# Two value chunks of an encoder block's input projection as one seven-product column block, with q, k and v kept in DRAM

## The chip, the core and the metric

The kernel runs on one core of a Trainium2 chip. The metric is the device time of one execution in microseconds. Before the change three runs took 2026.24, 2027.93 and 2028.84; the median is 2027.93.

The core has TensorE (PE in the profile: matmuls and transposes, with PEld its weight load), VectorE (DVE), ScalarE (ACT), GpSimd (POOL) and SyncE (SP, which here only issues transfers). Each engine works through its own instructions in the order in which they are written; engines wait for each other by semaphores. Transfers are issued from the queues of SP, ACT and POOL. Matmuls write to PSUM, which has 8 banks of 128 partitions x 512 floats.

## The reference

One layer of an encoder on x of 512 tokens x 2048, all in float32:

```
h = rmsnorm(x, g_mix)
qa, ka, va, qb, kb, vb = split(h @ w_in)         # 8 + 2 + 2 heads of 128 (A), 8 + 8 + 8 heads (B)
a = rmsnorm(mixer_a(qa, ka, va))                  # per-head rms norm of q and k, 2-D axial rotary, softmax
b = rmsnorm(mixer_b(qb, kb, vb))                  # rotary on 32 of 128 dims, three dilated windows merged
x = x + concat(a, b) @ w_out
x = x + swiglu(rmsnorm(x), w_gate_up, w_down)     # inner width 5632
out = rmsnorm(x, g_final)
```

w_in has 4608 columns: qA at 0 (1024 wide), kA and vA at 1024 (256 each), qB at 1536, kB at 2560 and vB at 3584 (1024 each).

## The kernel before, in words

Precision: every float32 factor of a matmul is split into a high part (ScalarE copies it to a rounded type, `split_hi`, line 235) and a low part (VectorE subtracts, `split_lo`, line 240). `mm3` (lines 197 to 199) then makes three matmuls: high x high, high x low, low x high.

Units: the whole program is a list `units`. A plain unit is one 128-row slice of 512 weight columns for all four token tiles: 4 x 3 = 12 matmuls of 512 columns. A plain chunk (`in_chunk`, `add_chunk`) is 16 units with four PSUM banks. The main loop at the end goes through the units; for each it issues loads and weight splits some way ahead (`prepare`: loads up to 24 us of planned time ahead, splits up to 10), then the unit's matmuls, then what hangs on it (`post`, `hooks`), and then takes one task from a list `side`. So the order of every engine's queue is written out by this loop; the durations in it (`UNIT_US`, `COLS_US`) only set how far ahead things are issued.

Stages: (1) in the first chunk (kA and vA) x is loaded in 128-column pieces and transposed on TensorE one step ahead of its use (`x_transposes`); the result is multiplied by g_mix and split to `xT`, and its square is added up on GpSimd, from which eight one-column matmuls (`col_sums`) and a power on GpSimd give the row scale r1. (2) Eight more plain chunks follow: qA (2), vB, two of q and k of B, vB, two more of q and k. Each is evicted from PSUM with the row scale to tiles that stay in SBUF. (3) As soon as q, k, v of a head exist, its attention goes to `side`, one task a unit: transposes of q (`tq`) and k (`tk`), four scores, four transposes of probabilities (`pt`), four products with v (`pv`). For a chunk of qA there are first eight tasks of norm and rotary (`push_norm_rope`, two for each token tile) and two empty tasks. (4) Eight output chunks of 8 units, A then B, with residual and the sums for the next norm. (5) Gate and up projection in 11 column blocks, (6) down projection in 6, and the last norm.

Column block (`ColBlock`): for two weight column groups of 512 and the two halves of the tokens, seven products of a Strassen-Winograd kind (m1 to m7) take the place of eight. A unit (`Cols`) is one product for one pair of 128-row slices: 2 x 3 = 6 matmuls. Before the split VectorE forms sums of weights for four of the seven products (`weights`, line 771); the stationary side, sums of the activations, lies ready in `arena`. Splits of such a unit (lines 734 and 737) go to eight `twins`, so at most eight units ahead. The products accumulate in banks named z, y and x, and are evicted between them. Before the change only stages 5 and 6 use it.

`RAWS` is the number of weight tiles that may be loaded at once for each kind of block.

Of the kernel before, what the change touches and what calls it, by code (L numbers as in the profile page):

```python
# [50 lines left out]
RAWS = {"raw": 6, "craw": 24, "craw40": 23, "draw6": 22, "draw8": 28}  # L51
# [4 lines left out]
EVICT = 6  # L56

# [6 lines left out]
def encoder_block(ctx, tc, x, g_mix, w_in, g_q_a, g_k_a, g_out_a, g_out_b, w_out, g_ffn,  # L64
# [6 lines left out]
    sm = ctx.enter_context(tc.tile_pool(name="small", bufs=1))  # L71
# [14 lines left out]
    def wslot(tag):  # L86
        if tag == "wa":
            ring[0] += 1
            return home(16 + ring[0] % 12)
        return sp.tile([P, 512], F32R, tag=tag, bufs=W_TILES[tag], name=nm("w"))  # L90
# [4 lines left out]
    def small(base, n=4):  # L95
        return sm.tile([P, 16], F32, tag="t", bufs=24, name=nm(base))[:, :n]
# [7 lines left out]
    ident = cp.tile([P, P], F32, name="ident")  # L104
    gm = cp.tile([P, KD], F32, name="gm")
    gf = cp.tile([P, KD], F32, name="gf")
    go = cp.tile([P, KD], F32, name="go")
    mask = cp.tile([P, S + S - P], F32, name="mask")
    ropeb = cp.tile([P, 2, NT, PARTIAL], F32, name="ropeb")
    ones = cp.tile([P, 1], F32, name="ones")  # L110
    mhalf = cp.tile([P, 16], F32, name="mhalf")
    gqk = cp.tile([P, 2, HD], F32, name="gqk")
# [5 lines left out]
    def home(n):  # L118
        return form_tile(n % 7, n // 7).rearrange("p a b -> p (a b)")
# [5 lines left out]
    warm = slot("warm", BF16, (P, 512))  # L125
# [26 lines left out]
    def load_consts():  # L152
        for i, g in enumerate((g_q_a, g_k_a)):
            nc.sync.dma_start(gqk[:, i, :], row_bcast(g, HD))
        yield
# [3 lines left out]
        yield  # L159
        nc.sync.dma_start(ropeb, c_partial)  # L160
        yield
        nc.sync.dma_start(mask, c_mask)
        yield
# [9 lines left out]
    def rsqrt_mean(ss, n, count, name):  # L173
        t = small(name + "m", n)
        nc.vector.tensor_scalar(t, ss, 1.0 / count, EPS, op0=OP.mult, op1=OP.add)
        r = small(name, n)
        nc.gpsimd.tensor_tensor(r, t, mhalf[:, :n], op=OP.pow)
        return r

    def split(src, name, gain=None, between=None, at=None):  # L180
        if at is None:
            hi, lo = slot(name + "h", F32R), slot(name + "l", F32R)
        else:
            hi, lo = home(at), home(at + 1)
# [3 lines left out]
        else:  # L188
            nc.scalar.activation(hi, src, AF.Copy, scale=gain)
            if between is not None:  # L190
                between()
# [62 lines left out]
    xT = [None] * KD  # L254
    ssx = slot("ssx")

    def x_transposes(k):
        ps = bank("xt")
        for t in range(NT):
            nc.tensor.transpose(ps[:, t * P:(t + 1) * P], xs[k][:, t, :], ident)  # L260
        if k == 0:
            xT[k] = split(ps, "xT", gm[:, k:k + 1], at=0)
            nc.scalar.activation(ssx, ps, AF.Square)
        else:
            sq = slot("xsq")
            xT[k] = split(ps, "xT", gm[:, k:k + 1], lambda: nc.scalar.activation(sq, ps, AF.Square), 2 * k)
            nc.gpsimd.tensor_tensor(ssx, ssx, sq, op=OP.add)
# [9 lines left out]
    def make_r1():  # L277
        r1["r"] = rsqrt_mean(col_sums(ssx), NT, D, "r1")
        r1["rs"] = small("r1s")
# [4 lines left out]
    def push_tables():  # L284
        for i, name in enumerate(("k", "q")):
# [15 lines left out]
            side.extend(lambda a=a, f=part: f(a) for a in range(3))  # L301

    def push_norm_rope(q0, dst, t, nh, name):
# [3 lines left out]
        def first():  # L307
            gs = tabs[name][1]
            tmp = st["tmp"] = slot("ra")
            ss = small("ssq")  # L310
# [4 lines left out]
            st["rs"] = rsqrt_mean(ss[:, :nh], nh, HD, "rq")  # L315
# [7 lines left out]
        def second():  # L323
            gc = tabs[name][0]
# [5 lines left out]
        side.extend((first, second))  # L330

    qA, kA, kTA, vA = {}, [], {}, {}
    vB, qkB = {}, {}
    kTA_done = []

    def post_kvA(ps):
        for j in range(2):
            vA[j] = tuple(home(48 + 2 * j + i).rearrange("p (a b) -> p a b", a=2) for i in range(2))
        for t in range(NT):
            r = r1["r"][:, t:t + 1]  # L340
            k0 = slot("kA")
            src = ps[t][:, 256:]
            h, l = vA[t // 2]
            nc.scalar.activation(h[:, t % 2, :], src, AF.Copy, scale=r)
            nc.scalar.activation(k0[:, :256], ps[t][:, :256], AF.Copy, scale=r)
            nc.vector.scalar_tensor_tensor(l[:, t % 2, :], src, r, f32(h[:, t % 2, :]), op0=OP.mult, op1=OP.subtract)
            kA.append(k0)
        for t in range(NT):
            push_norm_rope(kA[t][:, :256], kA[t][:, 256:], t, NKV, "k")
        wait(1)  # L350
        for kv in range(NKV):
            side.append(lambda kv=kv: transpose_k_a(kv))

    def transpose_k_a(kv):
# [3 lines left out]
        kTA[kv] = split(ps, "kT", at=52 + 2 * kv)  # L358

    def post_qA(j, ps):  # L360
        for t in range(NT):
            q0 = slot("qA")
            nc.scalar.activation(q0, ps[t], AF.Copy, scale=r1["r"][:, t:t + 1])
            push_norm_rope(q0, q0, t, 4, "q")
            qA[j, t] = q0
        wait(2)
        for h in range(4):
            push_head(("A", 4 * j + h))

    def post_vB(j, ps):  # L370
        for t in range(NT):
            r = r1["r"][:, t:t + 1]
            h, l = home(32 + 2 * (NT * j + t)), home(33 + 2 * (NT * j + t))
            nc.scalar.activation(h, ps[t], AF.Copy, scale=r)
            nc.vector.scalar_tensor_tensor(l, ps[t], r, f32(h), op0=OP.mult, op1=OP.subtract)
# [753 lines left out]
```

## Time and profile before

| | us |
|---|---|
| median of three runs | 2027.93 |
| the profiled execution | 2026.94 |
| its span, first to last instruction | 2025.2 |
| TensorE busy | 2005.7 |
| VectorE busy | 1474.1 |
| ScalarE busy | 1051.6 |
| GpSimd busy | 134.9 |

The span is that of one profiled execution. A group's row gives line, engine, operation, output and inputs, count, then busy time and the mean in ns of one. A row of the timeline gives start and duration in us, then engine, line, operation, count, and in brackets how long the engine had been idle and who ended it. A row of a window gives the window, its length, then for PE, PEld, DVE, ACT and POOL the busy time with the number of instructions, then TensorE's granted clock, the share of the 16 DMA engines and GB/s. Neighbouring instructions of one engine overlap a little, so starts tell more of the rate than durations. A row of waits gives who waited for whom, us in total, times, and the longest.

### The profile page before, as it was taken

The page shows a single profiled execution, that of the slowest core. Times are in us where ns is not written, and L with a number is a line of the kernel's source. Part 1 is how long each engine was busy: PE and PEld are TensorE (multiplying, and loading weights), DVE is VectorE, ACT ScalarE, POOL GpSimd, SP SyncE. Part 2 cuts the span into 40 slices and gives each one's busy share as a digit, 9 for nine tenths or more (in the row PEclk, how much of TensorE's full clock was granted, in tenths as well). Part 3 has the DMA queues.
Part 4 walks back from the last instruction along what each step waited for, and adds up shares of the span by engine and source line. Part 5 has one row for each costly group of instructions (what it writes and reads, how often), then busy time and mean ns, then how long its engine had stood idle before and what let it go on. Part 6 is the DMA issues. An engine that isn't in the chain of part 4 may idle for free. (4 is left out here: it accounts for less than half of the span.)

```text
span 2025.2 us, 26727 instructions
## 1 busy us (share of the span) xinstructions
PE 2005.7 (99%) x9123; PEld 1652.5 (82%) x9123; DVE 1474.1 (73%) x2596; ACT 1051.6 (52%) x1872; POOL 134.9 (7%) x149
## 2 busy tenths in 40 slices
PE   9999999999999999999999999999999999999997
PEld 7888888888888888888888888888888887788885
DVE  5555755554754688878877878878779987887876
ACT  5324344443543565555555555555556665666655
POOL 3100100000000000000000000000000121111121
PEclk9999999999999999999999999999999999999998
DMA  7322322223433546657558567467477799768754
GB/s 236 106 80 70 98 74 73 79 78 96 147 113 130 205 142 217 206 167 267 193 195 267 166 222 255 152 221 253 153 253 254 207 248 265 205 158 256 212 124 165
DMA packets 210360, 354.90 MB, mean 175 GB/s; under 512 B 19072, under 2 KB 63920, under 8 KB 210224
## 3 DMA queue, kind: packets, MB, share of 16 engines
q1 hardware_dynamic: 189440, 304.10, 45.9%
q0 software_dynamic: 12544, 25.17, 7.0%
q10 hardware_dynamic: 8240, 23.93, 3.5%
q8 instruction: 71, 1.16, 0.2%
q14 instruction: 65, 0.53, 0.1%
HBM read 300.97 MB, written 52.17 MB: 174 GB/s over the span
## 5 line engine op out<-in xcount | busy, mean ns | idle before, releaser
L734 ACT ACTIVATE tw<-raw 128x512 fp32r<-128x512 f32 x924 | 559.3, 628 | 442.5 <-DVE raw L771 280.7
L737 DVE TENSOR_TENSOR tw<-raw,tw 128x512 fp32r<-128x512 f32 x924 | 619.1, 686 | 173.4 <-ACT tw L734 169.5
L197 PE MATMUL zc<-tw,arena 128*128 128x512 f32 x1056 | 416.1, 394 | 2.0 <-ACT ev L907 1.9
L198 PE MATMUL zc<-tw,arena 128*128 128x512 f32 x1056 | 413.6, 392 | 3.5 <-DVE tw L737 3.5
L199 PE MATMUL zc<-tw,arena 128*128 128x512 f32 x1056 | 413.1, 391 | 0.0
L771 DVE TENSOR_TENSOR raw<-raw,raw 128x512 f32<-128x512 f32 x528 | 361.3, 684 | 0.5 <-DMA raw<-in_w_gate_up_dram 0.5
L198 PEld LDWEIGHTS zc<-tw,arena 128*128 128x128 f32 x1056 | 199.3, 189 | 46.7 <-DVE tw L737 6.5
L197 PEld LDWEIGHTS zc<-tw,arena 128*128 128x128 f32 x1056 | 199.1, 189 | 43.9 <-ACT ev L907 3.0
L199 PEld LDWEIGHTS zc<-tw,arena 128*128 128x128 f32 x1056 | 199.1, 189 | 41.5
L197 PE MATMUL pj<-w,arena 128*128 128x512 f32 x576 | 229.0, 398 | 1.2 <-ACT w L235 1.2
L198 PE MATMUL pj<-w,arena 128*128 128x512 f32 x576 | 224.8, 390 | 0.9 <-DVE w L240 0.9
L199 PE MATMUL pj<-w,arena 128*128 128x512 f32 x576 | 225.5, 391 | 0.1
L198 PE MATMUL yc<-tw,arena 128*128 128x512 f32 x528 | 206.0, 390 | 0.8 <-DVE tw L737 0.8
L197 PE MATMUL yc<-tw,arena 128*128 128x512 f32 x528 | 206.8, 392 | 0.0
L199 PE MATMUL yc<-tw,arena 128*128 128x512 f32 x528 | 205.8, 390 | 0.0
L240 DVE TENSOR_TENSOR w<-raw,w 128x512 fp32r<-128x512 f32 x176 | 130.8, 753 | 21.4 <-ACT w L235 13.6
L908 POOL DMA_DIRECT2D x1d<-ev x76 | 67.4, 990 | 1155.3 <-ACT ev L907 1149.4
L235 ACT ACTIVATE w<-raw 128x512 fp32r<-128x512 f32 x176 | 106.5, 627 | 56.1 <-PE pj L199 32.0
L199 PEld LDWEIGHTS pj<-w,arena 128*128 128x128 f32 x576 | 108.2, 188 | 23.9 <-DVE arena L192 0.5
L197 PEld LDWEIGHTS pj<-w,arena 128*128 128x128 f32 x576 | 108.3, 188 | 23.6 <-ACT w L235 1.4
L198 PEld LDWEIGHTS pj<-w,arena 128*128 128x128 f32 x576 | 108.5, 188 | 23.2 <-DVE w L240 1.2
L198 PEld LDWEIGHTS yc<-tw,arena 128*128 128x128 f32 x528 | 99.2, 188 | 21.8 <-DVE tw L737 1.6
(189 smaller groups left out, 2539.0 us busy)
## 6 DMA issues: line engine op xcount, KB each, us to landing
raw<-in_w_gate_up_dram SPq DMA_DIRECT2D x616, 256.0 KB, 4.5
raw<-in_w_down_dram SPq DMA_DIRECT2D x176, 256.0 KB, 6.7
forms<-pair SPq DMA_DIRECT2D x22, 896.0 KB, 5.2
raw<-in_w_in_dram SPq DMA_DIRECT2D x38, 512.0 KB, 3.7
x1d<-ev POOLq DMA_DIRECT2D x76, 256.0 KB, 6.6
fr<-forms ACTq DMA_DIRECT2D x35, 512.0 KB, 4.5
raw<-in_w_in_dram SPq DMA_DIRECT2D x68, 256.0 KB, 3.0
raw<-in_w_out_dram SPq DMA_DIRECT2D x32, 512.0 KB, 4.9
```

Source lines behind the costliest of these rows:

```text
L197: nc.tensor.matmul(dst, ah, bh, start=start, stop=False, skip_group_check=chained)
L198: nc.tensor.matmul(dst, ah, bl, start=False, stop=False, skip_group_check=chained)
L199: nc.tensor.matmul(dst, al, bh, start=False, stop=stop, skip_group_check=chained)
L235: nc.scalar.activation(self.w[0], src, AF.Copy)
L240: nc.vector.tensor_tensor(self.w[1], self.src, f32(self.w[0]), op=OP.subtract)
L734: nc.scalar.activation(self.pair[:, 0], self.src, AF.Copy)
L737: nc.vector.tensor_tensor(self.pair[:, 1], self.src, f32(self.pair[:, 0]), op=OP.subtract)
L771: nc.vector.tensor_tensor(t[dst], t[src[0]], t[src[1]], op=OP.add if form == "m6" else OP.subtract)
L908: nc.gpsimd.dma_start(x1_dram[2 * cb + j, row], e, accum_op=OP.add)
```

## The change

Input projection: after the first plain chunk (kA, vA) the two chunks of vB become one column block (`in_block`), with the order of products m1, m2, m7, m6, m5, m4, m3. Then come six plain chunks: qA (2) and four of q and k of B. For the block the activations' sums are needed, so in the first chunk each transposed x is copied to a tile (`xpair`, three buffers, one for a pair of steps), split into `arena`, and two steps after the second of a pair VectorE makes four sums and, a step later, ScalarE and VectorE split two of them (`x_sums`, `x_split`). One of these overwrites a quarter of x, which is saved to DRAM by POOL's queue before (`ar_dram`) and brought back after m7.

Row scale: the squares are taken on ScalarE from x loaded once more in rows (`load_rows` in steps 8 to 11, two buffers of 1 MB; `row_squares` in steps 11 to 14). The squares on ScalarE and their sum on GpSimd for each step, and the eight column-sum matmuls, go.

q, k, v: every chunk is evicted and stored to DRAM (`spill`) and loaded again by SP's queue when attention needs it (`reload`, `load_vB`); the split of v is made then.

Attention: all heads are one list. Each task is a slot s: transposes of the probabilities of slot s - 6, product with v of slot s - 7, score of slot s, and the q and k transposes of the head of slot s + 3. Each task has a cost; a unit gives 1.13 credit during the remaining plain chunks and 1.6 during A's output chunks, and tasks are taken while the credit lasts. The tables, k and v of A come after the block, the rest after the first chunk of qA.

Small tiles are packed into fewer buffers, and `RAWS` is 21 in place of 23 and 22 for the last gate and up block and the first down blocks.

```diff
-RAWS = {"raw": 6, "craw": 24, "craw40": 23, "draw6": 22, "draw8": 28}
+RAWS = {"raw": 6, "craw": 24, "craw40": 21, "draw6": 21, "draw8": 28}
+HEAD_RATE = (1.13, 1.6)
+TURN_LAG = 6
+COLUMN_BLOCKS = 1
...
-            xT[k] = split(ps, "xT", gm[:, k:k + 1], at=0)
-            nc.scalar.activation(ssx, ps, AF.Square)
+            nc.scalar.activation(hi, ps3, AF.Copy, scale=gain)
+            nc.vector.scalar_tensor_tensor(lo, ps3, gain, f32(hi), op0=OP.mult, op1=OP.subtract)
+            nc.scalar.activation(flat, ps, AF.Copy, scale=gain)
         else:
-            sq = slot("xsq")
-            xT[k] = split(ps, "xT", gm[:, k:k + 1], lambda: nc.scalar.activation(sq, ps, AF.Square), 2 * k)
-            nc.gpsimd.tensor_tensor(ssx, ssx, sq, op=OP.add)
+            nc.scalar.activation(flat, ps, AF.Copy, scale=gain)
+            nc.scalar.activation(hi, view, AF.Copy)
+            nc.vector.tensor_tensor(lo, view, f32(hi), op=OP.subtract)
+        if half == 0:
+            hook(k, lambda: nc.gpsimd.dma_start(ar_dram[:, i], arena[0][:, 1, i]))
+        else:
+            hook(k + 2, lambda: x_sums(i))
+            hook(k + 3, lambda: x_split(i))
+
+    def x_sums(i):
+        a_l, a_r, s3, s2, b_l, b_r, s1, s4 = (xpair[i][:, n * 256:(n + 1) * 256] for n in range(8))
+        form_sums(a_l, a_r, b_l, b_r, s1, s2, s3, s4)
+
+    def x_split(i):
+        parts = xpair[i].rearrange("p (f c) -> p f c", c=256)
+        for src, dst in ((parts[:, 2:4], arena[0][:, 1:3, i]), (parts[:, 6:8], arena[1][:, 2:4, i])):
+            nc.scalar.activation(dst[:, :, 0], src, AF.Copy)
+            nc.vector.tensor_tensor(dst[:, :, 1], src, f32(dst[:, :, 0]), op=OP.subtract)
...
+    def load_rows(t):
+        rows[t] = sp.tile([P, D], F32, tag="rows", bufs=2, name=nm("rows"))
+        nc.sync.dma_start(rows[t], x[0, t * P:(t + 1) * P, :])
+
+    def row_squares(t):
+        nc.scalar.activation(rows[t], rows[t], AF.Square, accum_out=ss1[:, t:t + 1])
...
-        r1["r"] = rsqrt_mean(col_sums(ssx), NT, D, "r1")
+        r1["r"] = rsqrt_mean(ss1, NT, D)
...
+    def post_plain(name, ps):
+        for t in range(NT):
+            e = slot("ev" + name)
...
+                nc.scalar.activation(e, ps[t], AF.Copy, scale=r1["r"][:, t:t + 1])
+            store(name, t, e, nc.scalar)
+
+    def reload(name, dst):
         for t in range(NT):
+            dst[t] = slot(name)
+            nc.sync.dma_start(dst[t], spill[name][t])
...
+        def task(s):
+            head, i = at(s - TURN_LAG)
+            if head:
+                head.pt(i)
+            head, i = at(s - TURN_LAG - 1)
+            if head:
+                head.pv(i)
...
+            head, i = at(s)
+            if head:
+                head.score(i)
+            head, i = at(s + 3)
+            if head and i == 0:
+                head.tq()
+            if head and i == 1:
+                head.tk()
+        cost = 1.5 if spec[0] == "A" else 1.2
...
+        first = light(0.5, table_tasks() + kn)
+        todo = [weighed(0.1, lambda: reload("qA0", qA[0]))] + light(0.8, q_tasks(0))
+        for h in range(8):
+            todo += head_tasks(("A", h))
...
+    def in_block(names, lo):
+        first = not blocks
+        box = ColBlock(w_in, 0, lo, KD // 2, REREAD, "craw",
+                       chain=("m1", "m2", "m7", "m6", "m5", "m4", "m3") if first else CHAIN)
...
+        rows_of("m1", 0, 0, begin)
+        rows_of("m7", 1, 1, begin)
+        rows_of("m6", 1, 0, begin)
+        rows_of("m2", 0, 0, close)
+        rows_of("m5", 1, 1, close)
+        rows_of("m4", 1, 0, close)
+        rows_of("m3", 0, 1, only)
...
+    last.after("m7", 1, lambda: nc.gpsimd.dma_start(arena[0][:, 1], ar_dram))
+    last.after("m5", 0, load_consts)
+    last.after("m5", 3, lambda: reload("kvA", kA))
+    last.after("m3", 0, lambda: side.extend(first_tasks))
...
+            if 8 <= n < 8 + NT:
+                load_rows(n - 8)
+            if 11 <= n < 11 + NT:
+                row_squares(n - 11)
             if n == KD - 1:
                 make_r1()
             if n + 1 < KD:
-                x_transposes(n + 1)
+                x_prep(n + 1)
...
-        if side:
-            side.popleft()()
+        credit = credit + HEAD_RATE[n >= attend[1]] if attend[0] <= n < attend[2] else 1.0
+        while side and credit >= getattr(side[0], "cost", 1.0):
+            f = side.popleft()
+            credit -= getattr(f, "cost", 1.0)
+            f()
+        if not side:
+            credit = 0.0
```

`begin` evicts a bank with the row scale on ScalarE, `close` adds a second bank to it on VectorE and stores it by POOL's queue, `only` evicts and stores by ScalarE's.

More of the change, by code (lines that the diff above doesn't have):

```diff
@@ L252, in wait, with x_of, x_prep @@
         side.extend([lambda: None] * n)
-    xT = [None] * KD
-    ssx = slot("ssx")
-    def x_transposes(k):
+    xpair = [None] * (KD // 2)
+    ar_dram = dp.tile([P, KD // 2, 2, 256], F32R, tag="ar", name="ar")
+    def x_of(k, t):
+        m = (0, 1, 3, 4)[2 * (k % 2) + t // 2]
+        return cols(tuple(form_tile(m, k // 2)[:, j] for j in range(2)), (t % 2) * P)
+    def x_prep(k):
         ps = bank("xt")
@@ L329, in second @@
                                     st["rs"][:, :, None].to_broadcast([P, nh, HD]), op=OP.mult)
-        side.extend((first, second))
-    qA, kA, kTA, vA = {}, [], {}, {}
+        return [first, second]
+    qA, kA, kTA, vA = {}, {}, {}, {}
     vB, qkB = {}, {}
[L334 to L338, printed above, removed]
-        for t in range(NT):
[L340 to L347, printed above, removed]
-        for t in range(NT):
[L349 to L352, printed above, removed]
+    spill = {name: dp.tile([NT, P, 512], F32, tag=name, name=name)
+             for name in ("kvA", "qA0", "qA1", "vB0", "vB1", "qkB0", "qkB1", "qkB2", "qkB3")}
@@ new lines, in reload, with split_vA @@
+    def reload(name, dst):
+        assert stored[name] == NT, name
+        for t in range(NT):
+            dst[t] = slot(name)
+            nc.sync.dma_start(dst[t], spill[name][t])
+    def split_vA(t):
+        if not vA:
+            for j in range(2):
+                vA[j] = tuple(place(2, 2 * j + i).rearrange("p (a b) -> p a b", a=2) for i in range(2))
+        h, l = (v[:, t % 2, :] for v in vA[t // 2])
+        src = kA[t][:, 256:]
+        nc.scalar.activation(h, src, AF.Copy)
+        nc.vector.tensor_tensor(l, src, f32(h), op=OP.subtract)
@@ new lines, in encoder_block @@
+    last.after("m5", 0, load_consts)
+    last.after("m5", 3, lambda: reload("kvA", kA))
+    last.after("m3", 0, lambda: side.extend(first_tasks))
+    last.after("m3", 0, twins.clear)
+    first_tasks, later_tasks = attention_tasks()
+    attend = [len(units)]
+    queue = side.extend
+    for names, lo in groups[COLUMN_BLOCKS:]:
+        for name, c in zip(names, lo):
+            in_plain(name, c)
+            if queue:
+                hook(len(units) if name == "qA0" else attend[0], lambda: side.extend(later_tasks))
+                queue = None
```

484 lines of the change are left out of this document (263 added, 221 removed).

## The prediction

> **What bounds the kernel now.** First I read the page's head and its busy times, then the windows of the half that the change touches.
>
> ```profile
> span 2025.2 us, 26727 instructions
> PE 2005.7 (99%) x9123; PEld 1652.5 (82%) x9123; DVE 1474.1 (73%) x2596; ACT 1051.6 (52%) x1872; POOL 134.9 (7%) x149
> 300.00:325.00 25.00, 25.00 (x122) 20.66 (x121) 13.35 (x24) 9.97 (x21) 1.29 (x1) 1.00 0.25 74
> 625.00:650.00 25.00, 25.00 (x112) 20.73 (x111) 11.45 (x18) 6.79 (x11) 0.00 (x0) 1.00 0.27 85
> ```
>
> TensorE (PE, first pair of numbers) is busy in both stretches, at a granted clock of 1.00, while VectorE (DVE) and ScalarE (ACT) have room. So in this half a matmul taken away is time gained, unless TensorE then waits for someone. Its own spacing comes from the timeline; between the first two rows lie 45 steps. The other rows are the last step of the first chunk and its end.
>
> ```profile
> 639.67 0.39 PE L198 MATMUL pw<-w,arena 128*128 128x512 f32 x1
> ...
> 649.87 0.39 PE L198 MATMUL pw<-w,arena 128*128 128x512 f32 x1
> 51.55 0.60 PE L260 MATMUL xt<-ident,x 128*128 128x128 f32 x4
> 54.75 0.60 PE L260 MATMUL xt<-ident,x 128*128 128x128 f32 x4
> 55.10 0.48 PE L197 MATMUL pj<-w,arena 128*128 128x512 f32 x1
> 55.65 0.40 PE L199 MATMUL pj<-w,arena 128*128 128x512 f32 x1
> 58.05 1.05 PE L272 MATMUL cs<-ones,ssx 128*128 128x1 f32 x8
> 58.96 0.47 PE L197 MATMUL pj<-w,arena 128*128 128x512 f32 x1
> ```
>
> (649.87 - 639.67) / 45 = 0.2267 us for one matmul of 512 columns. A plain unit has 12 (2.72 us), a unit of a column block 6 (1.36 us), a step of the first chunk with its transposes 3.20 us. What TensorE waited for is short, and the head has two rows of it:
>
> ```profile
> PE pj L197 <- ACT w L235: 1.2, 1, 1.2
> PE pj L198 <- DVE w L240: 0.9, 1, 0.9
> ```
>
> **What is taken away.** Two plain chunks are 2 x 16 x 12 = 384 matmuls; the block has 7 products x 8 pairs x 6 = 336. 48 fewer make 48 x 0.2267 = 10.9 us. The eight column-sum matmuls go too, since the squares are now summed along rows: from 58.05 to 58.96, 0.9 us. The 2.1 us of waits above came behind the old square of x on ScalarE, which is gone; the new copy of x takes its place there. Between 0 and 2.1 I take 1.0. Gains: 12.8 us.
>
> **ScalarE in the first chunk.** Per step it now copies the transposed x (a dependent pair with its high part) and splits a weight, and every second step splits two sums. Then come four squares of 128x2048, in steps 11 to 14, each queued ahead of the next x.
>
> ```profile
> 53.25 0.63 ACT L235 ACTIVATE w<-raw 128x512 fp32r<-128x512 f32 x1
> 55.38 0.69 ACT L189 ACTIVATE arena<-xt,gm 128x512 fp32r<-128x512 f32 x1 [1.50 <-PE xt L260]
> 56.45 1.15 ACT L235 ACTIVATE w<-raw 128x512 fp32r<-128x512 f32 x2
> L689 ACT ACTIVATE arena<-pair 128x1024 fp32r<-128x1024 f32 x8 | 8.4, 1045 | 0.0
> L582 ACT ACTIVATION_READ_ACCUMULATOR j<-x 128x1 f32 x16 | 3.0, 186 | 0.0
> ```
>
> Two independent splits take 1.15, so one adds 0.52. A step costs 0.69 + 0.63 + 0.1 between them + 0.52 + (2 x 0.52) / 2 = 2.46 of 3.20. A square, by the slope from 0.63 (512) to 1.05 (1024), is 0.63 + 3 x 0.42 + 0.19 = 2.08. Four steps then need 4 x 4.54 = 18.2 against 12.8: 5.4 late. How much lateness is free? A step's transposes start at 54.75 and ScalarE 0.63 later, at 55.38; its 0.69 and 0.63, VectorE's 0.69 (next rows) and two hand-overs of 0.1 end 2.84 after the transposes' start. The first matmul that reads the low part is the third of its step, one step on (55.65 for the transposes of 51.55, 4.10): 1.25 free. VectorE's rows:
>
> ```profile
> 53.50 1.30 POOL L267 TENSOR_TENSOR ssx<-ssx,xsq 128x512 f32<-128x512 f32 x1 [1.92 <-ACT xsq L266]
> 54.06 1.28 DVE L240 TENSOR_TENSOR w<-raw,w 128x512 fp32r<-128x512 f32 x1
> 60.44 0.17 DVE L280 TENSOR_SCALAR r1s<-r 128x4 f32<-128x4 f32 x1 [1.14 <-POOL r L177]
> 60.51 0.69 DVE L240 TENSOR_TENSOR w<-raw,w 128x512 fp32r<-128x512 f32 x1
> 658.98 1.56 DVE L660 TENSOR_TENSOR pair<-pair 128x256 f32<-128x256 f32 x4 [3.62 <-ACT pair L682]
> ```
>
> Per two steps it has two low parts of x, two of weights and two of sums at about 0.60 to 0.69 each, and 1.56 of sums: 5.3 of 6.4. But only three pair buffers exist, so the copy of x for step 2i+6 waits for the last split of pair i, and VectorE stands still during copy and high part (1.4): a loop of 5.3 + 1.4 = 6.7, 0.3 more than 6.4, five times; the free 1.25 takes the first two or so, 0.6 stays. TensorE waits 5.4 - 1.25 + 0.6 = 4.7. Bounds: 2.5 (squares run in ScalarE's idle time before their step) to 7 (no slack).
>
> Without POOL's add the weight split is 0.69, not 1.28; I used 0.69. The Trainium skill (GPSIMD Engine Reference, 1. Specifications) says that GpSimd shares its SBUF interfaces with VectorE and contends with two-input instructions, which agrees with these rows; if the eight POOL transfers that now save a half of x did the same, 8 x 0.59 = 4.7 us more of VectorE would come into this chunk. The trace has a split in the middle of two such issues, and it is not stretched:
>
> ```profile
> 1641.58 1.77 POOL L908 DMA_DIRECT2D x1d<-ev  x2 [6.14 <-ACT ev L907]
> 1642.41 0.69 DVE L737 TENSOR_TENSOR tw<-raw,tw 128x512 fp32r<-128x512 f32 x1 [3.36 <-ACT tw L734]
> ```
>
> **From the first chunk into the block.** The row scale now comes after the last square, by way of VectorE's queue and POOL's power (the 1.14 above), so the four evictions start some 1.0 after the chunk's end. Each is 0.69 plus a store issued on ScalarE (0.33, below): 4 x 1.05 = 4.2. Behind them stands the split of the block's fifth unit; only four units of 1.36 (5.4) are split ahead, where before three or four of 2.72 were. High part at 5.2 + 0.6, low part at 6.5, wanted at 5.4 + 0.23: 0.9. Then VectorE still owes two pairs' remains (1.56 + 4 x 0.60 = 4.0) among units that leave it 1.36 - 0.60 = 0.76 each: 4.0 less 3 x 0.76 is 1.7. Together 2.6; bounds 0 and 4. In the block m5 follows m6 in the same banks, so its first matmul waits for the eviction: 0.69 + 0.1 + the matmul's end, less the other bank's 0.68, is 0.4; bound 1.7, the longest such wait below.
>
> **From the block into attention.** q of the first chunk is no longer roped from the eviction but stored, loaded, and then roped. Rows for eviction, store, load and the old rope work:
>
> ```profile
> 104.65 2.73 ACT L363 ACTIVATE qA<-pj,r 128x512 f32<-128x512 f32 x4 [8.16 <-PE pj L199]
> 105.37 0.29 DVE L312 CUSTOM_DVE_ANT_0 ra<-qA 128x128 f32<-128x128 f32 x1 [6.32 <-ACT qA L363]
> 110.42 0.28 DVE L312 CUSTOM_DVE_ANT_0 ra<-qA 128x128 f32<-128x128 f32 x1
> 124.95 1.29 DVE L240 TENSOR_TENSOR w<-raw,w 128x512 fp32r<-128x512 f32 x2
> 133.69 0.60 PE L419 MATMUL qt<-ident,qA 128*128 128x128 f32 x4
> L474 ACTq DMA_DIRECT2D oA<-oT x8: 326/326/357, 178.7 to 383.8; - x8
> oA<-oT ACTq DMA_DIRECT2D x8, 256.0 KB, 2.2
> oback<-oA SPq DMA_DIRECT2D x8, 256.0 KB, 3.0
> ```
>
> The eviction can start 1.8 before the chunk's end F (nine matmuls, less the drain). First store issued at F - 1.1, landed F + 1.1, load landed F + 4.2 to 4.4. VectorE's queue stands at the first rope task until then. A row of q, with two weight splits of 0.60 (1.29 for two, less the overlap) among it, took 110.42 - 105.37, so 3.85 alone; four rows with five weight splits between them are 18.4: done at F + 22.8. The tasks go out at 1.13 per unit and cost 0.8, so the first head's transposes come after the seventh unit, F + 19.0 (before, ten units: 104.65 + 1.8 + 27.2 = 133.7, as the row says). TensorE waits 3.8; bounds 0 and 7 (a load that lands 3 later). The weight splits behind the rope arrive within 0.1 of their need, so nothing else.
>
> For the rest of attention matmuls and transposes are the same, and the cycle uses each probability block six slots after its score. A plain unit with 0.75 slot is about 2.72 + 0.75 x 1.9 = 4.1 of TensorE against VectorE's 0.75 x 2 + 0.6: covered. The old order, with a shorter lag, shows no TensorE wait in this stretch, so I take 0 and move neither end. The tasks weigh about 115, the units give 80 x 1.13 + 32 x 1.6 = 142: the queue empties before B's output chunks. The new reloads are at most 256 KB each where the DMA share is 0.25: 0.
>
> **The smaller weight buffers** (23 to 21, 22 to 21) act in the down projection, where loads are already late:
>
> ```profile
> 1697.74 0.63 ACT L734 ACTIVATE tw<-raw 128x512 fp32r<-128x512 f32 x1 [4.96 <-DMA raw<-in_w_down_dram]
> PE zc L197 <- ACT ev L907: 1.9, 2, 1.7
> ```
>
> One buffer fewer issues a load about a unit (1.36) later, and what ScalarE waits there it hands on in part, since splits run up to eight units ahead. I take 0.5; bounds -1 (another order of loads) and +4 (most of a wait like this one again).
>
> **Sum.** -12.8 + 4.7 + 2.6 + 0.4 + 3.8 + 0.5 = -0.8. The profiled execution took 2026.94 (1.7 around its span); so 2026.1, and as the median of the runs before (2027.93) stands 1.0 above it, 2027.1. All low ends give -10.9 - 0.9 - 2.1 + 2.5 - 1 = -12.4, all high ends -10.9 - 0.9 + 7 + 4 + 1.7 + 7 + 4 = +11.9.
>
> **Rivals.**
> Absorbed waits (faster): rope and block start cost nothing because VectorE gets there in time. For it: the old order left TensorE without a wait at 133.69, and VectorE is at 13.35 of 25 in the attention window. Against: the rope can't start before q is back. -0.8 - 3.8 - 2.6 = -7.2: 2020.7.
>
> The row loads come late (slower). They are four of 1 MB on SP's queue in steps 8 to 11; only two buffers exist, so the third waits for the first square, the fourth for the second, and the block's first weights queue behind them.
>
> ```profile
> raw<-in_w_in_dram SPq DMA_DIRECT2D x12, 512.0 KB, 5.3
> 0.00:60.00 60.00, 56.12 (x268) 43.57 (x269) 34.09 (x47) 30.50 (x56) 20.20 (x20) 1.00 0.70 215
> ```
>
> At 215 GB/s a 512 KB load moves in 2.4 of its 5.3, which leaves 2.9 of landing, and 1 MB moves in 4.9: the third lands 7.8 after its issue, where ScalarE wants it after about 7; the fourth, behind it and two weight loads (2.4), at 4.9 + 2.4 + 4.9 + 2.9 = 15.1, where it is wanted at 11.1 and the first lateness moves that to 11.8: 3.3 late, and ScalarE holds the next x behind it. The weights behind them I put another 3 late. It decides once the fourth lands later than its step, and gives -0.8 + 6.3 = +5.5: 2033.4. Against: 215 is a mean over a window in which the DMA engines were 0.70 busy. The Trainium skill (DMA: Bandwidth & Descriptors, Anatomy of one DMA) gives 2.0 us plus bytes at 436 GB/s, an estimate of 4.4 us for 1 MB: by that the fourth would be in time and this rival void. No row shows a 1 MB load.
>
> The smaller buffers cost a whole late load (slower): +5 in place of 0.5, the 4.96 once more and unshared: 2031.6. Against it: one or two buffers of more than twenty go.
>
> That the change doesn't do what it says (products not fewer) is excluded by the count.
>
> **Chances.** About 0.2%, 4 us, is what can be told from no change. Forecast 0.38 (its own range 2023 to 2031; 0.03 of it faster, 0.02 slower by over 4), absorbed 0.32, late rows 0.24, buffers 0.06 (half of it over 4). So faster 0.35, same 0.36, slower 0.29. The 8-in-10 range, pulled in a little from the two sums of ends, is 2016.5 to 2038.
>
> **What would show it.** Right: 48 fewer 512-column matmuls, gaps of ScalarE's making on TensorE in steps 11 to 14, about 3 us of gaps in the first eight units of the block, one gap of 3 to 4 us before the first q transposes, ended by VectorE. Wrong: a first chunk as even as before's 3.20 a step; ScalarE waiting for row loads; gaps inside the head cycle, which I price at nothing; a longer wait for weights around 1700.

## The result, and the profile after

Five runs of the changed kernel took 2035.35 to 2041.53 us, median 2039.54; five of the kernel before 2026.24 to 2029.18, median 2027.93. The ratio is 1.0055, 95% interval 1.0041 to 1.0070: the change makes the kernel slower by about 11.6 us. The median lies above the range of the prediction (2016.5 to 2038). The profiled execution took 2039.54, with a granted TensorE clock of 0.996 (before: 0.997).

The head of the page after the change:

```profile
span 2037.8 us, 27271 instructions
PE 2004.7 (98%) x9067; PEld 1642.6 (81%) x9067; DVE 1522.5 (75%) x2706; ACT 1093.7 (54%) x1928; POOL 123.2 (6%) x149
```

TensorE has 56 instructions fewer (48 matmuls and 8 column sums), as counted beforehand, and its busy time fell by 1.0, not by 11.8. Where the rest went shows in windows over the part that the change touches. They are cut at the first chunk's end, the first q transposes of after and the output chunks. Columns as in the prediction: window, length, then busy time and count for PE, PEld, DVE, ACT, POOL, then clock, DMA share, GB/s. Before:

```profile
5.00:62.00 57.00, 54.69 (x268) 43.59 (x267) 34.96 (x47) 30.39 (x58) 20.39 (x16) 1.00 0.69 211
62.00:120.00 58.00, 58.00 (x260) 48.02 (x261) 35.54 (x109) 19.05 (x35) 6.26 (x7) 1.00 0.35 100
120.00:225.00 105.00, 105.00 (x495) 86.90 (x494) 55.84 (x112) 42.29 (x89) 2.35 (x2) 1.00 0.25 76
225.00:480.00 255.00, 255.00 (x1213) 210.90 (x1213) 142.81 (x335) 105.17 (x221) 14.60 (x12) 1.00 0.26 81
480.00:625.00 145.00, 145.00 (x696) 119.81 (x695) 83.13 (x173) 68.22 (x135) 9.13 (x7) 1.00 0.43 138
```

And after:

```profile
5.00:62.00 57.00, 54.67 (x259) 42.75 (x258) 37.62 (x71) 45.07 (x74) 4.46 (x8) 1.00 0.93 313
62.00:120.00 58.00, 54.54 (x234) 43.19 (x233) 50.12 (x88) 33.19 (x55) 2.76 (x4) 1.00 0.72 250
120.00:225.00 105.00, 101.86 (x450) 83.93 (x449) 60.92 (x165) 30.25 (x57) 9.44 (x12) 0.98 0.46 157
225.00:480.00 255.00, 253.55 (x1217) 208.32 (x1216) 154.86 (x350) 121.41 (x253) 14.93 (x12) 1.00 0.33 107
480.00:625.00 145.00, 138.30 (x648) 109.79 (x647) 90.43 (x203) 70.03 (x140) 10.43 (x8) 0.98 0.49 158
```

Length less TensorE's busy time is its idle time: before 2.3 in the first window and nothing behind it; after 2.3, 3.5, 3.1, 1.5 and 6.7. Two clocks read 0.98: there some matmuls also ran at half rate (below), which a busy column hides. The largest loss stands in the last window. It holds the end of the input projection and A's output chunks, with heads of B's attention between them: matmuls that the change does not touch. The longest of the waits of after's TensorE up to 660 us name who was late; in the whole list no wait behind the first matmul is ended by a transfer:

```profile
PE qt L474 <- DVE qkB L453: 3.4, 5, 1.2
PE qt L474 <- DVE qA L383: 3.1, 1, 3.1
PE zc L203 <- DVE tw L691: 2.5, 3, 1.9
PE pj L202 <- ACT arena L284: 2.2, 2, 1.2
PE kt L484 <- DVE qTl L194: 1.5, 2, 0.7
```

The first row is the rotary step (here called rope) of B's q and k (`qkB`) on VectorE, ahead of the transposes of q (`qt`). The timeline shows the worst instance:

```profile
532.53 0.16 DVE L502 RECIPROCAL smalls<-smalls 128x1 f32<-128x1 f32 x1 [0.88 <-ACT p L501]
...
533.13 0.35 DVE L449 TENSOR_TENSOR turning<-qkB,fixed 128x64 f32<-128x64 f32 x2
...
534.19 0.33 PE L474 MATMUL qt<-fixed,qkB 128*128 128x128 f32 x1 [1.18 <-DVE qkB L453]
535.12 0.33 PE L474 MATMUL qt<-fixed,qkB 128*128 128x128 f32 x1 [0.60 <-DVE qkB L453]
536.03 0.48 PE L474 MATMUL qt<-fixed,qkB 128*128 128x128 f32 x1 [0.59 <-DVE qkB L453]
536.61 0.29 DVE L453 TENSOR_TENSOR qkB<-qkB,turning 128x128 f32<-128x128 f32 x1
536.96 0.47 PE L474 MATMUL qt<-fixed,qkB 128*128 128x128 f32 x1 [0.45 <-DVE qkB L453]
538.09 0.63 PE L204 MATMUL pw<-arena,arena 128*128 128x512 f32 x1
...
541.92 0.63 PE L204 MATMUL pw<-arena,arena 128*128 128x512 f32 x1
```

The four ropes run from 533.13 to 536.90, 3.8 us, and each transpose stands in TensorE's queue until its own is done: 1.18 + 0.60 + 0.59 + 0.45 = 2.8 us in four waits. VectorE itself had stood idle for 0.88 shortly before (first row), so it was the order of its queue that kept the ropes until then. Then comes what no step of the prediction had: between the last two rows lie nine steps, so (541.92 - 538.09) / 9 = 0.426 us a matmul, not 0.227. The windows around it give the clock:

```profile
210.00:216.00 6.00, 5.29 (x17) 4.22 (x18) 3.15 (x5) 1.64 (x3) 0.00 (x0) 0.72 0.27 84
532.00:537.00 5.00, 2.19 (x9) 0.99 (x8) 4.16 (x19) 2.11 (x5) 0.00 (x0) 0.89 0.27 92
537.00:543.00 6.00, 6.00 (x18) 4.73 (x19) 4.22 (x9) 1.81 (x4) 0.00 (x0) 0.52 0.00 0
543.00:548.00 5.00, 5.00 (x29) 4.14 (x27) 3.08 (x7) 3.50 (x7) 1.29 (x1) 1.00 0.31 105
```

From 537 to 543 TensorE counts as busy all the time, and gets half its clock.

The whole stretch from the first matmul of the input projection to the first of gate and up can be added up from TensorE's timeline, row by row: start to start, less 0.2267 for each matmul of 512 columns; what a row puts down to another engine is a wait, and a spacing of 0.40 to 0.45 without one is half rate.

| us | before | after | difference |
|---|---|---|---|
| matmuls: 2880, 2832 | 652.8 | 641.9 | -10.9 |
| transposes and column sums | 44.3 | 46.2 | +1.9 |
| waits | 2.1 | 16.7 | +14.6 |
| the rest of a gap that has a wait | 0.3 | 3.4 | +3.1 |
| half rate | 0.0 | 3.6 | +3.6 |
| small gaps that no wait explains | 16.4 | 19.7 | +3.3 |
| together | 715.9 | 731.6 | +15.7 |
| from there to the span's end | 1302.4 | 1299.3 | -3.1 |

Waits, rest and half rate by place, before and after: first chunk 2.4 and 2.7; block 0 and 4.0; first q of A 0 and 4.5; 225 to 480 us 0 and 1.7; 480 to 625 us 0 and 10.8. (The last line of the table takes the first `zc` matmul behind the output chunks, below, from the spans.)

```profile
722.77 0.39 PE L197 MATMUL zc<-tw,arena 128*128 128x512 f32 x1
```

```profile
738.48 0.39 PE L202 MATMUL zc<-tw,arena 128*128 128x512 f32 x1
```

So the theory to test: the block saves its 10.9, and the new order of the attention tasks loses about 12.5 in stalls of TensorE, about half of it where two tasks (ropes of B, transposes of B's q) stand too near each other at the quick pace of 1.6 credit a unit. Rivals: the block itself is to blame (ScalarE's squares, VectorE's backlog), or the 10.9 never arrives.

### The profile page after: what moved, and what is told of

The parts are those of the page before. It is cut to its first block, busy times and chain, and to the rows that moved or that the text cites. A ratio compares the mean times of both kernels' runs of the same rounds, so it can differ in the third digit from the quotient of the medians.

```text
span 2037.8 us, 27271 instructions
## 1 busy us (share of the span) xinstructions
PE 2004.7 (98%) x9067; PEld 1642.6 (81%) x9067; DVE 1522.5 (75%) x2706; ACT 1093.7 (54%) x1928; POOL 123.2 (6%) x149
## 5 line engine op out<-in xcount | busy, mean ns | idle before, releaser
L688 ACT ACTIVATE tw<-raw 128x512 fp32r<-128x512 f32 x980 | 593.3, 628 | 467.2 <-DVE raw L725 309.5
L691 DVE TENSOR_TENSOR tw<-raw,tw 128x512 fp32r<-128x512 f32 x980 | 656.3, 687 | 173.4 <-ACT tw L688 169.4
L202 PE MATMUL zc<-tw,arena 128*128 128x512 f32 x1120 | 439.9, 393 | 3.0 <-ACT ev L1045 2.2
L203 PE MATMUL zc<-tw,arena 128*128 128x512 f32 x1120 | 437.7, 391 | 5.0 <-DVE tw L691 4.8
L204 PE MATMUL zc<-tw,arena 128*128 128x512 f32 x1120 | 437.1, 390 | 0.0
L725 DVE TENSOR_TENSOR raw<-raw,raw 128x512 f32<-128x512 f32 x560 | 383.3, 685 | 2.9 <-DMA raw<-in_w_gate_up_dram 2.9
L203 PEld LDWEIGHTS zc<-tw,arena 128*128 128x128 f32 x1120 | 210.6, 188 | 51.5 <-DVE tw L691 9.0
L202 PEld LDWEIGHTS zc<-tw,arena 128*128 128x128 f32 x1120 | 210.7, 188 | 47.6 <-ACT ev L1045 2.9
L204 PEld LDWEIGHTS zc<-tw,arena 128*128 128x128 f32 x1120 | 210.6, 188 | 43.9
L203 PE MATMUL yc<-tw,arena 128*128 128x512 f32 x560 | 218.3, 390 | 1.1 <-DVE tw L691 1.1
L202 PE MATMUL yc<-tw,arena 128*128 128x512 f32 x560 | 219.1, 391 | 0.0
L204 PE MATMUL yc<-tw,arena 128*128 128x512 f32 x560 | 218.1, 389 | 0.0
L202 PE MATMUL pj<-w,arena 128*128 128x512 f32 x448 | 179.0, 399 | 2.4 <-ACT arena L284 2.2
L203 PE MATMUL pj<-w,arena 128*128 128x512 f32 x448 | 175.7, 392 | 0.7 <-DVE w L245 0.7
L204 PE MATMUL pj<-w,arena 128*128 128x512 f32 x448 | 176.1, 393 | 0.0
L203 PEld LDWEIGHTS yc<-tw,arena 128*128 128x128 f32 x560 | 105.2, 188 | 23.8 <-DVE tw L691 2.4
L204 PEld LDWEIGHTS yc<-tw,arena 128*128 128x128 f32 x560 | 105.1, 188 | 22.0
L202 PEld LDWEIGHTS yc<-tw,arena 128*128 128x128 f32 x560 | 105.1, 188 | 21.5
L202 PE MATMUL xc<-tw,arena 128*128 128x512 f32 x280 | 109.2, 390 | 0.0
L203 PE MATMUL xc<-tw,arena 128*128 128x512 f32 x280 | 109.1, 389 | 0.1
L204 PE MATMUL xc<-tw,arena 128*128 128x512 f32 x280 | 109.0, 389 | 0.0
```

Of the source, the lines that this page charges most:

```text
L202: nc.tensor.matmul(dst, ah, bh, start=start, stop=False, skip_group_check=chained)
L203: nc.tensor.matmul(dst, ah, bl, start=False, stop=False, skip_group_check=chained)
L204: nc.tensor.matmul(dst, al, bh, start=False, stop=stop, skip_group_check=chained)
L688: nc.scalar.activation(self.pair[:, 0], self.src, AF.Copy)
L691: nc.vector.tensor_tensor(self.pair[:, 1], self.src, f32(self.pair[:, 0]), op=OP.subtract)
L725: nc.vector.tensor_tensor(t[dst], t[src[0]], t[src[1]], op=OP.add if form == "m6" else OP.subtract)
```

## The experiments

SBUF is so full that most edits only fit with fewer weight tiles for the new block (`craw`). So the control has 20 in place of 24, and every kernel below has it too. Each ratio is to runs of the kernel before on the same chip at the same time; kernels of different groups are compared by these ratios. The first four ran together, the next four, and the last four.

**Control.**

```diff
-RAWS = {"raw": 6, "craw": 24, "craw40": 21, "draw6": 21, "draw8": 28}
+RAWS = {"raw": 6, "craw": 20, "craw40": 21, "draw6": 21, "draw8": 28}
```

> The changed kernel with 20 instead of 24 weight tiles for the column blocks; nothing else. It is the control for the next three, which need the memory. Every theory: within 3 us of the changed kernel (2036.5 to 2042.5), the same TensorE gaps at 207 us (q of A) and between 500 and 605 us (B's heads in A's output chunks).

Measured: 2038.46, ratio 1.0054 (1.0039 to 1.0069), the same as with 24. Its last window:

```profile
480.00:625.00 145.00, 137.88 (x651) 109.52 (x650) 91.19 (x204) 69.93 (x141) 10.43 (x8) 0.99 0.48 156
```

**A steady pace.** The tasks behind the input projection go out at 1.13 a unit, not 1.6.

```diff
-HEAD_RATE = (1.13, 1.6)
+HEAD_RATE = (1.13, 1.13)
```

> As the control, but A's output chunks give 1.13 credit a unit like the plain chunks, not 1.6. Theory pace (B's heads are pushed faster than VectorE's chain of maximum, exponential, normalising and split can follow): the TensorE waits between 500 and 605 us, some 9.7 us, and the half-speed stretch behind them, 2.2 us, go; 2027 to 2030. Theory rope order (the rotary of B's q and k stands straight in front of the transposes that need it): the waits on the rotary, 3.9 us, and the half-speed stretch stay, 2.5 to 5 us are won from the other waits.

Measured: 2032.02, ratio 1.0025 (1.0013 to 1.0036), 6.4 under the control. Two views, the window and the waits:

```profile
480.00:625.00 145.00, 142.84 (x688) 115.81 (x688) 95.29 (x211) 74.36 (x149) 10.46 (x8) 1.00 0.48 155
```

```profile
PE qt L474 <- DVE qkB L453: 1.5, 3, 0.6
```

Idle time in that window fell from 7.1 to 2.2, 37 more TensorE instructions fit into it, and the clock is whole. VectorE does more work there than in the control (95.29 against 91.19), so over the window its throughput was not the limit, as the prediction held. What the slower pace widens is the distance in the queues: the worst transposes of q now start 2.2 us behind the first of their ropes, not 1.06, and wait 0.95, not 3.0. Neither theory on record came out whole: the waits for ropes shrank and did not go, most waits for split probabilities and k went too, and the time stayed above 2027 to 2030.

**A gap behind the first q.** A task that does nothing, weighed 3.4, stands between the ropes of A's first q and the first transposes.

```diff
-        todo = [weighed(0.1, lambda: reload("qA0", qA[0]))] + light(0.8, q_tasks(0))
+        todo = [weighed(0.1, lambda: reload("qA0", qA[0]))] + light(0.8, q_tasks(0)) + [weighed(3.4, lambda: None)]
```

> As the control, but three units without an attention task stand between the rotary of A's first q and its first transposes. Theory: the 3.3 us wait at 207 us goes, and with it the slow matmuls behind it (0.43 us spacing for about 4 us, another 1.9): 5 us faster. Rival (the wait's length is all it costs): 3.3 us faster. Rival (the wait only moves to the next consumer of VectorE): no change.

Measured: 2032.00, ratio 1.0028 (1.0019 to 1.0037), 6.5 under the control. The wait of 3.1 for q of A and the half rate behind it are gone; in its place stands one of 1.1 for a weight split of VectorE. Gate and up begins 6.8 earlier than in the control: 2.8 of that is this wait with its half rate, 1.3 other waits, 1.8 small gaps and transposes, and 0.9 lies ahead of the first input matmul, so it has nothing to do with the edit. The waits in A's output chunks stayed (7.8 against 7.1), on another tensor: the probabilities, up to 2.8 at once.

```profile
PE o L203 <- DVE pTl L194: 3.8, 2, 2.8
PE qt L474 <- DVE qkB L453: 2.0, 3, 1.2
```

**Ropes one slot earlier.**

```diff
-                todo += tasks[:1] + light(0.5, b_ropes(j)) + tasks[1:]
+                todo += light(0.5, b_ropes(j)) + tasks
```

> As the control, but the rotary of B's q and k of the next pair is one slot earlier in the list (before slot 0 of an odd head, not between slots 0 and 1). Theory rope order: the four waits of 2.8 us at 532 to 537 us, the half-speed stretch of 2.6 us behind them, and the smaller one at 442 go: 5 to 6 us faster. Theory pace: VectorE is as late as before, the waits turn up at the probability splits instead, under 2 us won.

Measured: 2035.67, ratio 1.0042 (1.0026 to 1.0059), 2.8 under the control, within what the two intervals leave open, so a gain is not shown. The row `qt <- qkB` is gone; in its place stands

```profile
PE o L203 <- DVE pTl L194: 3.3, 5, 2.5
```

The ropes' 3.8 us of VectorE now delay the low part of a transposed probability block. At a pace of 1.6 they are in somebody's way in both places tried, which fits the larger effect of the pace.

**Squares of 64 columns.** One of the rival's suspects, ScalarE's squares of x, cut to a thirtieth. This kernel leaves most of the sum of squares out, so its row scale is not that of the layer.

```diff
-        nc.scalar.activation(rows[t], rows[t], AF.Square, accum_out=ss1[:, t:t + 1])
+        nc.scalar.activation(rows[t][:, :64], rows[t][:, :64], AF.Square, accum_out=ss1[:, t:t + 1])
```

> As the control with 20 weight tiles, but each of the four row squares reads 64 of 2048 columns (the row scale is then that of a part of x). The loads of the rows stay. Theory squares (my prediction: ScalarE is over-full in steps 11 to 14): the two waits in the first chunk, 2.2 us, go, and since the evictions start earlier the block's first waits shrink too; 3 to 5 us faster. Rival (the three pair buffers hold up the copy of x; the squares ran in idle time): under 1 us faster, the two waits stay.

Measured: 2036.30, ratio 1.0052 (1.0037 to 1.0067), no different from the control, where 3 to 5 us were expected. The waits in the first chunk went from 2.2 to 0, and a new one came at the block's start:

```profile
65.41 0.69 ACT L407 ACTIVATE evkvA<-pj,smalls 128x512 f32<-128x512 f32 x1 [2.60 <-DMA kvA<-evkvA]
...
67.18 0.49 PE L202 MATMUL zc<-tw,arena 128*128 128x512 f32 x1 [2.90 <-ACT tw L688]
```

An eviction of the first chunk waits for the store of an earlier one to land, and the block's weight split stands behind it on ScalarE. The squares do make their 2.2, but taking them away gains next to nothing: the next limit is as near.

**Sums of the last two pairs later.** The other suspect, VectorE's backlog at the block's start.

```diff
-            hook(k + 2, lambda: x_sums(i))
-            hook(k + 3, lambda: x_split(i))
+            late = 0 if i < 6 else (9, 10)[i - 6]
+            hook(k + 2 + late, lambda: x_sums(i))
+            hook(k + 3 + late, lambda: x_split(i))
```

> As the control, but the sums and splits of the last two pairs of x come nine to ten units later, when VectorE has room in m2. Theory backlog (VectorE's left-over work is what the block's first units wait for): the waits between 60 and 80 us, 2.4 us, fall under 0.8; 1.5 to 2.5 us faster. Rival (the evictions and stores on ScalarE are what they wait for): the waits stay, no change.

Measured: 2040.16, ratio 1.0069 (1.0053 to 1.0084), no faster. In its profile, the fastest of its four runs (2036.59), the waits at the block's start fell from 2.4 to 1.0, but the eviction between m6 and m5 now comes late:

```profile
108.80 1.25 ACT L765 ACTIVATE evvB<-zc,smalls 128x512 f32<-128x512 f32 x2
...
109.52 0.50 PE L202 MATMUL zc<-tw,arena 128*128 128x512 f32 x1 [2.55 <-ACT evvB L765]
```

**The three edits together** (pace, gap, ropes).

> As the control, with the three changes of before together: 1.13 credit in A's output chunks, three empty units before the first q transposes, the rotary one slot earlier. Theory (separate causes, each with its clock loss): the gains add up, 6 + 6 + 3 less an overlap of 2: 2024 to 2027, the same as the kernel before. Rival (one shared cause, VectorE's load): 2030 to 2032, no better than one of them alone.

Measured: 2024.31, ratio 0.9992 (0.9982 to 1.0002). From the control's 1.0054 that is 0.62%, 12.6 us; the three alone gave 0.29, 0.26 and 0.12%, together 0.67%. That fits separate waits whose costs add up, and not one shared limit (the rival's 2030 to 2032). The last window, and the same two operations as the worst instance of after:

```profile
480.00:625.00 145.00, 142.73 (x693) 116.14 (x692) 97.94 (x218) 78.31 (x156) 10.45 (x8) 1.00 0.48 156
```

```profile
L449 DVE TENSOR_TENSOR turning<-qkB,fixed x8: 214/218/222, 537.3 to 540.2; 128x64 f32<-128x64 f32 x8
L474 PE MATMUL qt<-fixed,qkB x4: 272/272/273, 543.6 to 543.9; 128*128 128x128 f32 x4
```

The first transpose now comes 6.3 us after the first rope, and TensorE waits for none of them. Yet waits, their rest and half rate in this window are 2.9, with the steady pace alone 2.7: others took the ropes' place, so here the pace is shown to matter and the ropes' own order is not.

**These three, with the later sums, and kA and vA stored by GpSimd's queue** (and the second set of q tasks weighed 1.0, not 0.8).

```diff
-            store(name, t, e, nc.scalar)
+            store(name, t, e, nc.gpsimd if name == "kvA" else nc.scalar)
```

> As the one before, and also the late sums of the last two pairs, the first chunk's stores on GpSimd's queue in place of ScalarE's, and cost 1.0 in place of 0.8 for the rotary of A's second q. Theory: block-start waits and the waits at 291 and 303 us go too, 3 to 4 us more: 2020 to 2024, faster than the kernel before. Rival: the waits are only moved, same as the one before.

Measured: 2024.58, ratio 0.9994 (0.9985 to 1.0004): nothing gained over the three edits. The wait of 2.5 between m6 and m5 is there again.

**No block.** B's value chunks are plain chunks again; the sums and splits for the block go, all else stays.

```diff
-    for names, lo in groups[:COLUMN_BLOCKS]:
-        in_block(names, lo)
...
+    for name, c in zip(*groups[0]):
+        in_plain(name, c)
```

> Control plus one part undone: B's two value chunks are again two plain chunks of 12 matmuls per unit behind the first chunk; the sums and splits of x for the block, and the copy of half of x kept in DRAM for it, go with it. All else (squares along rows, spilling, attention cycle) stays. 2880 matmuls in place of 2832: +10.9 us. Theory (the saving is real, the block's own costs are small): the waits at the block's start (3.2), the matmul behind the first eviction in the block (0.3) and about 1.0 of the waits in the first chunk go, so +6.4: 2044.5 against the control's 2038.5, with the waits of the attention cycle (505 to 605 us) at 7 as before. Rival (the block pays for itself only on paper, its own waits eat what it saves): within 2 us of the control, 2037 to 2040. Rival (the block costs nothing of its own): +10.9, 2049.

Measured: 2051.90, ratio 1.0125 (1.0110 to 1.0141), 0.71% or 14.4 over the control: more than any of the three expectations had it. Two windows and one row of the waits:

```profile
62.00:120.00 58.00, 58.00 (x258) 48.04 (x257) 16.50 (x25) 18.20 (x31) 0.00 (x0) 1.00 0.51 166
225.00:480.00 255.00, 249.65 (x1186) 204.18 (x1185) 149.50 (x337) 116.22 (x242) 14.94 (x12) 0.99 0.32 104
```

```profile
PE qt L469 <- DVE qkB L448: 6.4, 8, 1.7
```

The first chunk and the stretch behind it are as the theory had them: waits of 0.5 in all, where the control has 4.6. But the tasks now fall on other units, and the rope's four waits come twice: at 446 to 450 us, where the control has a single one of 0.59, and at 543 to 548. Waits, rest and half rate between 225 and 625 us are 20.3 against 12.3. In the two profiles the spans differ by 11.9 (2048.3 and 2036.4): +10.9 for the matmuls, -5.6 for what the first two windows lose (0.9 against 6.5, of which 0.8 is half rate at 8 to 12 us), +8.0 in the attention, and the remaining -1.4 mostly in small gaps. So the saving is real, but by these two profiles the block keeps only part of it, 10.9 - 5.6 - 1.4 = 3.9. That the rest of the attention cycle would stay as it is was wrong: where its tasks fall among the units decides as much as the block does.

**Squares behind the step's splits** on ScalarE (the control with one order changed).

```diff
-            if 11 <= n < 11 + NT:
-                row_squares(n - 11)
...
         prepare(n)
+        if 11 <= n < 11 + NT:
+            row_squares(n - 11)
```

> Control plus one order: each square of the rows is issued on ScalarE behind the copy and split of the next x and the weight splits of its step, not ahead of them. Theory of the prediction (a square holds the next x): the waits of 2.2 us before 60 us fall below 0.8, and the block's start stays at 2.4 to 3.5 since the last square is later by a step's work; -1 us, 2037.5. Rival (ScalarE is simply over-full there, order does not matter): waits of 2 us or more before 60 us, 2038.5.

Measured: 2041.53, ratio 1.0074 (1.0061 to 1.0087), no faster. The first chunk still waits 2.1, now at one stroke, and the block's start 4.0 in place of 2.4. ScalarE is over-full there whatever the order, as the rival had it.

**The three edits, with the stores on GpSimd's queue, without and with this order.**

> The three edits together (steady pace, gap behind the first q tasks, ropes ahead of the slot) plus the stores of the first chunk on GpSimd's queue in place of ScalarE's and the second set of q tasks at 1.0. Theory (the evictions of the first chunk wait for their stores to land, and ScalarE's issue of them costs 0.33 each): the waits of 3.2 between 60 and 80 us fall to about 1.5, so 2022.5 against 2024.3 of the three together. Rival (the splits of the last pairs on VectorE set this wait whatever the stores do): 2024.3, waits of 3 us there.

> As the run with the three edits and the stores on GpSimd's queue, with the squares of the rows behind the step's splits on ScalarE. Theory: waits before 60 us under 0.8 in place of 2.2, so 1 to 1.5 us less than that run: 2021. Rival (the wait moves to the block's start, as it did when the squares were cut): the same as that run within 0.5.

Measured: 2025.24, ratio 0.9992 (0.9983 to 1.0001), and 2024.16, ratio 0.9990 (0.9982 to 0.9999). The stores leave the waits at the block's start at 1.8 (the three alone: 1.5), and the time as it was, so the rival holds: they don't set it. With the order the waits before 60 us stay at 2.1, not under 0.8. The last kernel is the best of all, a tenth of a per cent under the kernel before; it can't be told from the three edits alone.

## Why the prediction was wrong

The step that failed is the attention cycle: "The old order, with a shorter lag, shows no TensorE wait in this stretch, so I take 0 and move neither end." It cost 12.5 (1.7 and 10.8 by place, above). Forecast and profile differ by 13.4 (-0.8 against the spans' +12.6), and since this term's ends were both put at 0, the range could not hold it. That the other terms leave only 0.9 is luck: they missed by 7.8 upwards (small gaps, transposes and column sums, block, q) and by 6.9 downwards (first chunk, down projection).

The argument compared VectorE's load with the time of a unit, and only at 0.75 slot a unit, the pace of A's heads (1.13 credit at a cost of 1.5). B's heads in A's output chunks go at 1.6 / 1.2 = 1.33 slots a unit, and no step works that stretch out. Even so the load over it was no limit (VectorE is busy for 90.43 of 145). What mattered was how near in the queues a result and its reader stand. In the kernel before, the ropes of B's last chunk stand in two tasks, with a unit for each and an empty one behind them (operation by operation, with the first and the last start):

```profile
L383 DVE TENSOR_TENSOR rope<-qkB,ropeb x8: 216/218/219, 530.0 to 534.2; 128x64 f32<-128x64 f32 x8
L419 PE MATMUL qt<-ident,qkB x4: 271/272/273, 536.2 to 536.6; 128*128 128x128 f32 x4
```

From the first rope to the first transpose are 6.2 us. After the change it is 1.06 (533.13 and 534.19), and TensorE was ready 1.18 before that: ahead of the first rope. The distance goes with the wait over all four groups of B's ropes in the changed kernel: 12.2, 2.5, 4.9 and 1.06 us from the first rope to the first transpose, and 0, 0.6, 0 and 2.8 of waits. Ropes and the half rate behind them make about half of the 12.5; the rest are shorter waits, mostly for the splits of k and of the probabilities, most of which the steady pace took away as well. The change moves the ropes directly ahead of the slot whose task transposes them, and such a move was priced for A's q and not for B's. The prediction did name the sign that would speak against it, gaps inside the head cycle.

Point by point:

- Fewer matmuls, -10.9: right. The column sums were to give another 0.9, but transposes and column sums together take 1.9 more, part of it in the stalls. Of the early waits 1.9 went, where 1.0 was taken.
- The squares, +4.7: measured 2.3 in two waits with what follows them (54.49 and 58.99 us), and 0.6 more in small gaps. The overload and its mechanism were right, the size was not:

```profile
42.87 1.90 ACT L318 ACTIVATE rows<-rows 128x2048 f32<-128x2048 f32 x1
...
55.70 1.92 ACT L318 ACTIVATE rows<-rows 128x2048 f32<-128x2048 f32 x1 [0.73 <-DMA rows<-in_x_dram]
...
58.99 0.50 PE L202 MATMUL pj<-w,arena 128*128 128x512 f32 x1 [1.20 <-ACT arena L284]
...
59.89 1.14 ACT L299 ACTIVATE arena<-xpair 128x512 fp32r<-128x512 f32 x2
...
63.37 0.69 ACT L407 ACTIVATE evkvA<-pj,smalls 128x512 f32<-128x512 f32 x1 [1.82 <-POOL smalls L184]
...
66.69 0.69 ACT L407 ACTIVATE evkvA<-pj,smalls 128x512 f32<-128x512 f32 x1 [0.40 <-PE zc L204]
...
72.73 0.50 PE L203 MATMUL zc<-tw,arena 128*128 128x512 f32 x1 [1.88 <-DVE tw L691]
```

  With the last splits of sums (59.89) four steps took 18.2, as forecast, though 0.73 of it is the wait for a row load. But these splits stand behind the high part for which TensorE waits; up to them it is 59.89 - 42.87 = 17.0, so ScalarE was 4.2 late, not 5.4; less the free 1.25 that is 2.9. The 0.6 for the three pair buffers did not show, and it doesn't follow from its own figures: five times 0.3 less the free 1.25 is 0.25, and the 1.25 had been spent on the squares already. Nor would it help to take the term away: with the squares nearly gone, the time stayed.
- The block's start, +2.6: 4.0 in the profile (3.2 of waits and 0.8 behind them), 3.4 in the control; at or near the upper end. The evictions came every 1.10 (63.37 to 66.69 are three steps; forecast 1.05), and the split behind them was late, then VectorE's, as described.
- m5 behind m6, +0.4: the matmul at the change of product came 0.49 after its neighbour, 0.26 more than usual. Right; the bound of 1.7 was too low for the run with later sums (2.55).
- q of A, +3.8: one wait of 3.1, where and by whom it was forecast, and 1.4 of half rate behind it. Right in its own terms; the price of the lost clock was in none of them.
- Smaller weight buffers, +0.5: from gate and up to the end the kernel was 3.1 quicker, and the waits there fell from 6.4 to 5.6. Nothing was lost; what made the rest of the 3.1 was not tested.
- Rivals: absorbed waits did not happen (block and q waited). Late row loads: the two of them with a landing on record took 8.3 and 5.1 us for 1 MB, where this rival had 7.8 and the estimate from the Trainium skill 4.4 (DMA: Bandwidth & Descriptors, Anatomy of one DMA; the fit there was measured on transfers that GpSimd issues, these are SyncE's). ScalarE waited once for rows, 0.73 (above), not 3.3, so the rival is void. Smaller buffers: void.

Not priced at all: half rate (3.6, counted in the places above), and small gaps that no wait explains (+3.3). In the run with the three edits, waits, their rest and half rate are still 11.2 above before (block and first chunk 5.5, q of A 1.3, attention 4.4) and small gaps 2.8: that uses up the 10.9, and the kernel comes level with the one before only by what it gains behind the output chunks.

## What to carry to other kernels

When a task is moved into an interleaved schedule, don't ask only whether its engine has time, and ask that at the pace of every stretch: list each producer that the move puts ahead of its reader, and the issue distance between them in the consumer's time; here 3.8 us of VectorE's work had 1.1 us of TensorE's time where it once had 6.2. Price a wait of 2 to 3 us on TensorE with the clock that it may cost: here up to 2.2 us more behind waits of 2.8 to 3.1. And before taking away a cause, look for the wait right behind it: cutting the squares and delaying the sums each removed the wait aimed at, and neither moved the time.

## What the runs showed of the hardware

After some waits, matmuls come at half rate for 2 to 5 us. The same wait for A's q, 3.1 us, was followed by it in seven of eight kernels that have it, each time for 5 to 11 matmuls at 0.426. Shorter waits did it too, not always:

| TensorE's wait | half rate followed |
|---|---|
| one of 3.1 (q of A) | in 7 of 8 kernels |
| 2.9 (block's start, squares cut) | yes |
| 2.8 (probabilities, with the gap) | yes |
| 2.7 to 3.5 in four pieces within 5 us (ropes) | in 5 of 6 kernels |
| 2.5 (between m6 and m5) | with later sums alone yes, with all edits no |
| 2.45 (probabilities, ropes one slot earlier) | yes |
| 1.95, 1.97, 2.10 (first chunk, three kernels) | yes |
| 1.88 (block's start, 72.73 above) | no |

The one kernel without it behind A's q and the ropes is that with later sums, whose profiled run is the fastest of its four (2036.59, median 2040.16).

The Trainium skill (TensorE: Matmul & The Clock Gate, Part 1: The HAM clock gate) says that the clock falls to half after at least one idle window of about 3.4 us, and that the window runs freely. The trace agrees with the half rate (0.426 here; the page gives 426.7 ns for 512 columns) and with a dependence on chance, but not with the length: single waits of 1.95 to 3.1 us were enough, and so was a set of four short ones with transposes between them.
